# Attention part of a diffusion mixer layer in program order: a hand-written order by arrival and by k-steps in place of the scheduler's

## The chip, the cores and the metric

The kernel runs on one core of one Trainium2 chip. The metric is the device time of one execution in microseconds; the reported time is the median of 3 runs. Engines by their short names: PE (TensorE, matmuls), DVE (VectorE), ACT (ScalarE), POOL (GpSimd), SP (SyncE, which issues the DMAs).

## The reference

One layer of a hybrid backbone on 1024 sample tokens (16 rows of 64) and 128 prompt tokens, width 1024, in float32:

```python
shift, scale, gate = split(silu(cond) @ w_ada + b_ada, 3)
h = rmsnorm(x, norm_g) * (1 + scale) + shift
q, k, v, z_a, u_b, z_b, u_c, z_c, g_a, g_b, g_c = split(h @ w_in)
q, k = rmsnorm(heads(q), q_g), rmsnorm(heads(k), k_g)
y_a = attend(q, k, v)          # 8 heads of 64
y_b = fft2(u_b, positions x channels).real @ w_fnet
y_c = pooled_minus_self(u_c) @ w_pool * pool_scale
merged = (sigmoid(g_a) * ((silu(z_a) * y_a) @ p_a) + sigmoid(g_b) * ((silu(z_b) * y_b) @ p_b)
          + sigmoid(g_c) * ((silu(z_c) * y_c) @ p_c))
out = x + gate * (merged @ w_o)
```

attend is, for the sample, attention over an 8 x 16 window of the grid with a relative bias, in one softmax with 128 cached keys; for the prompt, plain softmax attention. The new k and v of the prompt are outputs too. Sample and prompt have different cond.

## The kernel before, in words

The 1152 tokens are nine tiles of 128 (tiles 0 to 7 sample, 8 prompt); names end in the tile's number. Products that need float32's precision are made of three float16 matmuls of high and low parts (hh, hl for the normalised input; wh, wl for weights): `mm3`. A "k-step" is one such triple for one of the eight 128-row slices of the input width.

1. Start. SP loads sm, then in turn pieces of w_ada (wa0 to wa15), token tiles (xt), the first weights (wr_q). For each of three groups of token tiles, ACT squares them (xsq), POOL takes the root, DVE scales, PE transposes (xt into PSUM) and ACT copies to xT. `ada_piece` runs two k-slices of w_ada's rows; `ada_end` copies a row (ar on ACT), turns it with small matmuls (pb) and DVE forms sh and gs. `h_full` applies these to xT, `scale_h` finds a power-of-two scale (ab, pbd, m1h, pbs, hm, shs), `make_h` splits to hh (ACT) and hl (DVE). `head_scales` and `v_scales` bound the cached keys and values (km and vm on DVE; pkm, pks, pvm, pvs on PE).
2. Weights come by a generator (`prep_pair`, `prep_m`): load (wr), squares for a scale (wjk on ACT), a matmul over partitions (pw), wsc on DVE and POOL, then wh on ACT and wl on DVE. Who calls the generator's next step sets when each is issued.
3. Projection of q, k, v, by pairs of heads (four pairs). Per tile a PSUM bank p collects 8 k-steps. `p1_evac` squares (sq, ACT), sums (ss, DVE), takes the root and multiplies by the gain (rs, rg on POOL) and splits v. `p1_norm` multiplies (tk, DVE) and splits into tok (high part on ACT, low part on DVE). It is called one tile later through the list `late`. Pair 0's first five tiles ("early") run k by k with h being made.
4. Attention, 72 items (pair, head, row block or prompt, column block), software-pipelined: `stage_a` scores s, then sn with the bias and mn (DVE), `stage_b` exp (ACT) and ri (DVE), `stage_c` transposes (pt), pts high part (ACT) and low part (DVE), `stage_d` product po and yt (DVE), `stage_e` transpose to yT. Between the stages `fill` takes k-steps of the next pair from the generator `p1_tiles`; after pair 3 the k-steps are those of u (`u_tiles`). `group_q` and `group_k` transpose tokens to q and keys; bias tiles are made by POOL from gt and mk; SP makes vw and kb by copies. A list `ev` of step numbers says when each helper (pair_loads, pair_cached, next_step of the weights) is called.
5. After attention: z, the Fourier and pooling branches, gates and output. It is not edited but for its PSUM banks.

Each engine's order before is set by the tile scheduler, which places the instructions that the program gives it. PSUM has eight banks: p1 2, s 2, pt 2, po 2.

Of the kernel before, what the change touches and what calls it, by code (L numbers as in the profile page):

```python
# [20 lines left out]
P = 128  # L21
# [18 lines left out]
def mixer_layer(ctx: ExitStack, tc: tile.TileContext, xs, xp, smalls, qgrow, kgrow, bgate, wss, wgate, w1, w3, pw, wo,  # L40
# [27 lines left out]
    def squares(pool, raws, name):  # L68

        ss = pool.tile([P, len(raws)], F32, tag="wss", name=f"wss_{name}", bufs=3)  # L70
        for i, r in enumerate(raws):
            n = r.shape[-1]
            jk = pool.tile([P, 1024], BF16, tag="wjk", name=f"wjk_{name}{i}", bufs=1)
            S.activation(jk[:, :n], r, AF.Square, scale=1.0 / 16384, accum_out=ss[:, i:i + 1])
        return ss

# [4 lines left out]
    def scale_of(pool, ss, pk, name):  # L81


        n = ss.shape[-1]
        T.matmul(pk, onesp, ss, start=True, stop=True)
# [3 lines left out]
        G.tensor_tensor(sc_[:, 0:1], sc_[:, 2:3], mhalf[:, 0:1], op=ALU.pow)  # L89
        pow2(sc_[:, 0:1])  # L90
# [10 lines left out]
    def prep(pieces, name):  # L101
# [73 lines left out]
    with tc.tile_pool(name="hp", bufs=1, side="right") as hp:  # L175
# [23 lines left out]
        def m_ahead(i, c):  # L199
# [18 lines left out]
        with tc.tile_pool(name="qkv", bufs=1) as qkv:  # L218
# [6 lines left out]
            def new_pair(p, wu):  # L225
# [22 lines left out]
            def p1_evac(c, t, pt):  # L248
                p = c["p"]
                sq = qkv.tile([P, 256], F32, tag="sq", name=f"sq{p}_{t}", bufs=1)  # L250
                S.activation(sq, pt[:, :256], AF.Square, scale=c["i8"])
                ss = qkv.tile([P, 4], F32, tag="ss", name=f"ss{p}_{t}", bufs=3)
                V.reduce_sum(ss, sq.rearrange("p (g d) -> p g d", d=64), axis=AX.X)
                rs = qkv.tile([P, 4], F32, tag="rs", name=f"rs{p}_{t}", bufs=3)
                G.tensor_scalar(rs, ss, EPS, None, op0=ALU.add)
                G.tensor_tensor(rs, rs, mhalf, op=ALU.pow)  # L256
                rg = qkv.tile([P, 4, 64], F32, tag="rg", name=f"rg{p}_{t}", bufs=2)
                G.tensor_tensor(rg, c["g"], rs.unsqueeze(2).to_broadcast([P, 4, 64]), op=ALU.mult)  # L258
# [7 lines left out]
                return rg  # L266

            def p1_norm(c, t, pt, rg):
                p = c["p"]
                tk = qkv.tile([P, 256], F32, tag="tk", name=f"tk{p}_{t}", bufs=2)  # L270
                tkv = tk.rearrange("p (g d) -> p g d", d=64)
                V.tensor_tensor(tk, pt[:, :256], rg.rearrange("p g d -> p (g d)"), op=ALU.mult)  # L272
# [7 lines left out]
                V.tensor_tensor(t16[:, :, 1], tkv, t16[:, :, 0], op=ALU.subtract)  # L280
                c["toks"][t] = t16

            late = []

            def p1_tiles(c, tiles, wu):

                p = c["p"]
                for t in tiles:
                    pt = bank({8: "po", 6: "s"}.get(t, "p1") if p == 0 else "p1", f"p1_{p}_{t}")
                    for k in range(KT):  # L290
                        p1_mm(pt, t, wu, k, k == 0, k == KT - 1)
                        if k == 6 and late:
                            p1_norm(*late.pop())
                        if k == KT - 1:
                            late.append((c, t, pt, p1_evac(c, t, pt)))
                        yield


            with tc.tile_pool(name="st", bufs=1) as st:
# [15 lines left out]

                pc = bank("po", "pc")
# [1286 lines left out]
```

## Time and profile before

| | us |
|---|---|
| median of 3 runs (lowest, highest) | 1007.76 (1006.62, 1008.19) |
| the profiled execution's own time | 1007.29 |
| its span in the trace | 1005.5 |
| PE busy in the span | 913.6 |
| DVE, ACT, POOL busy | 651.4, 490.6, 207.0 |
| granted clock of PE, mean | 0.971 |

A busy time is the sum of an engine's instructions in the span. The span leaves out 1.8 us of the execution. Rows of a trace give the start in us from the span's start, the duration, the engine, the line, output<-inputs, and in brackets how long the engine was idle before and what released it. A granted clock of 0.50 is half the full one.

### The profile page before, as it was taken

To read this page: it belongs to the slowest core of one execution; us is meant where nothing else is said; L and a number is where in the kernel's file an instruction comes from. 1 tells how busy PE (TensorE), PEld (TensorE's weight loads), DVE (VectorE), ACT (ScalarE), POOL (GpSimd) and SP (SyncE) were. 2 spreads that over 40 slices of the span, in tenths; PEclk is the share of its full clock that TensorE was granted. 3 is DMA by queue.
4 is the path that set the end of the run, shared out by engine and by line. 5 is a ranking of instruction groups with operands and counts; after the bars stand their busy time and mean duration, and the time that the engine had idled before them with its cause. 6 is when DMAs were issued, how large, how long until landed. Compare 5 with 4: busy or idle time off the path is not lost.

```text
span 1005.5 us, 17517 instructions
## 1 busy us (share of the span) xinstructions
PE 913.6 (91%) x6526; PEld 676.4 (67%) x6526; DVE 651.4 (65%) x1446; ACT 490.6 (49%) x1017; POOL 207.0 (21%) x354
## 2 busy tenths in 40 slices
PE   5649688888889999989989999999999999999998
PEld 1325345556556666656788669888888888877886
DVE  1246546677666665398564649888888879766322
ACT  3484546656566665446344634564545544442100
POOL 0001534544444321022200230003011030100000
PEclk9768789999999999999999999999999999999999
DMA  7733231330411321512299712363434432228321
GB/s 301 284 119 89 65 96 42 101 78 25 104 51 43 82 87 53 171 44 74 63 310 295 264 40 94 114 199 118 145 102 130 132 107 86 61 73 301 107 83 52
DMA packets 71174, 120.28 MB, mean 120 GB/s; under 512 B 11520, under 2 KB 40108, under 8 KB 71089
## 3 DMA queue, kind: packets, MB, share of 16 engines
q1 hardware_dynamic: 71089, 119.17, 37.4%
q8 instruction: 51, 0.84, 0.3%
q14 instruction: 34, 0.28, 0.1%
HBM read 85.84 MB, written 26.75 MB: 112 GB/s over the span
## 4 chain that ended last, share of the span: by engine, by line
PE 62%; DVE 13%; POOL 8%; DMA 6%; ACT 6%; issue 3%; SPq 2%; ACTq 0%; DVEq 0%; POOLq 0%
PE wo L144 3%; PE wo L146 3%; PE wo L145 3%; POOL rs L256 3%; PE xc L146 3%; PE xb L144 3%; PE xb L145 3%; PE xb L146 3%; PE xc L144 3%; PE xc L145 3%; PE xa L144 3%; PE xa L146 3%; PE xa L145 3%; POOL rg L258 2%; PE ppa L144 2%
## 5 line engine op out<-in xcount | busy, mean ns | idle before, releaser
L144 PE MATMUL p<-wh_q,hh 128*128 128x384 f16 x288 | 97.5, 339 | 4.9 <-DVE tk L272 4.9
L145 PE MATMUL p<-wl_q,hh 128*128 128x384 f16 x288 | 97.5, 338 | 0.0
L146 PE MATMUL p<-wh_q,hl 128*128 128x384 f16 x288 | 97.0, 339 | 0.0
L674 ACT ACTIVATE sn<-sn,mn 128x512 f32<-128x512 f32 x64 | 46.4, 725 | 26.7 <-DVE mn L663 26.0
L144 PE MATMUL wo<-woh,mh 128*128 128x512 f32 x144 | 56.8, 395 | 1.1 <-ACT woh L1319 1.1
L145 PE MATMUL wo<-wol,mh 128*128 128x512 f32 x144 | 56.6, 393 | 0.0
L146 PE MATMUL wo<-woh,ml 128*128 128x512 f32 x144 | 56.5, 392 | 0.0
L687 DVE TENSOR_TENSOR pts<-pt,pts 128x512 f16<-128x512 f32 (+1 forms) x72 | 46.0, 639 | 13.0 <-ACT pts L686 13.0
L272 DVE TENSOR_TENSOR tk<-p,rg 128x256 f32<-128x256 f32 x36 | 15.2, 424 | 53.6 <-POOL rg L258 53.6
L703 PE MATMUL po<-vw,pts 128*128 128x64 f16 x576 | 33.1, 193 | 17.4 <-DVE pts L687 13.3
L703 PEld LDWEIGHTS <-pts 128*128 128x128 f16 x792 | 33.7, 98 | 22.4 <-DVE pts L687 15.8
L663 DVE CUSTOM_DVE_ANT_0 sn<-s,bias 128x512 f32<-128x512 f32 x64 | 43.8, 684 | 5.6 <-PE s L659 5.5
L1485 DVE TENSOR_TENSOR yo<-wo,gb 128x512 f32<-128x512 f32 x18 | 12.4, 691 | 51.3 <-PE wo L146 51.3
L144 PEld LDWEIGHTS <-hh 128*128 128x128 f16 x288 | 29.3, 102 | 23.1 <-DVE tk L272 5.3
L88 POOL TENSOR_SCALAR wsc_g<-wsc_g 128x1 f32<-128x1 f32 x12 | 2.8, 230 | 203.8 <-DVE wsc_g L87 203.8
L279 ACT CAST tok<-tk 128x256 f16<-128x256 f32 x36 | 14.6, 405 | 60.1 <-DVE tk L272 60.0
L146 PEld LDWEIGHTS <-hl 128*128 128x128 f16 x288 | 29.1, 101 | 20.6 <-issue 3.0
L146 PEld LDWEIGHTS <-wl_m 128*128 128x128 f16 x288 | 28.2, 98 | 21.0 <-DVE wl_m L99 2.6
L684 PE MATMUL pt<-ident,sn 128*128 128x128 f32 x256 | 38.8, 274 | 3.7 <-DVE pts L687 3.2
L145 PEld LDWEIGHTS <-hh 128*128 128x128 f16 x288 | 29.1, 101 | 18.5 <-issue 3.1
L144 PEld LDWEIGHTS <-wh_m 128*128 128x128 f16 x288 | 28.7, 100 | 18.0 <-issue 1.3
L145 PEld LDWEIGHTS <-wh_m 128*128 128x128 f16 x288 | 28.2, 98 | 17.4 <-issue 0.5
(656 smaller groups left out, 3058.0 us busy)
## 6 DMA issues: line engine op xcount, KB each, us to landing
wa<-in_wss_dram SPq DMA_DIRECT2D x16, 512.0 KB, 8.4
wr_q<-in_w_dram SPq DMA_DIRECT2D x16, 384.0 KB, 3.8
wr_m<-in_w_dram SPq DMA_DIRECT2D x24, 256.0 KB, 3.0
pp_c<-pec SPq DMA_DIRECT2D x24, 192.0 KB, 4.9
pp_b<-peb SPq DMA_DIRECT2D x24, 192.0 KB, 2.9
pp_a<-pea SPq DMA_DIRECT2D x24, 192.0 KB, 1.8
ppxc<-pp_c SPq DMA_DIRECT2D x16, 288.0 KB, 3.0
ppxb<-pp_b SPq DMA_DIRECT2D x16, 288.0 KB, 3.0
```

The source lines that it names most:

```text
L144: T.matmul(out, lh, rh, start=first, stop=False)
L145: T.matmul(out, lh, rl, start=False, stop=False)
L146: T.matmul(out, ll, rh, start=False, stop=last)
L256: G.tensor_tensor(rs, rs, mhalf, op=ALU.pow)
L258: G.tensor_tensor(rg, c["g"], rs.unsqueeze(2).to_broadcast([P, 4, 64]), op=ALU.mult)
L272: V.tensor_tensor(tk, pt[:, :256], rg.rearrange("p g d -> p (g d)"), op=ALU.mult)
L279: S.copy(t16[:, :, 0], tkv)
L663: V.tensor_tensor_reduce(out=sn, in0=pS, in1=bt.rearrange("p a b -> p (a b)"), op0=ALU.add, op1=ALU.min, scale=1.0, scalar=3e38, accum_out=mn)
L674: S.activation(e[:, :n], it["sn"], AF.Exp, bias=it["mn"], scale=-1.0, accum_out=sm_)
L684: T.transpose(pt[:, j * P:(j + 1) * P], it["e"][:, j * P:(j + 1) * P], ident)
L687: V.tensor_tensor(pts[:, 1, :n], pt[:, :n], pts[:, 0, :n], op=ALU.subtract)
L703: T.matmul(po[:, :64], it["pts"][:, a, j * P:(j + 1) * P], it["vl"][j][:, c_ * 64:(c_ + 1) * 64], start=(j == 0 and i == 0), stop=(j == nk ...
```

## The change

From the start of the projection stage to the end of attention, a `manual_schedule` block makes each engine take its instructions in the order of the program, and that program is rewritten:

- The start is written out by the order in which data is to arrive. Copies of x go to DVE and ACT by turns, ar3 stands behind two casts wh_q, not four; `head_scales` and `v_scales` come in the early tiles after k = 2 and 3; the generator of weights yields after each square, matmul and root.
- `p1_evac`, `p1_norm` and `late` become `p1_done` with a clock of k-steps (`tick`, `later`): roots (ss, rs, rg) 1 step after a tile, tk `wait` steps after (8 for pair 0, 6 for the others), tok's parts 1 and 2 steps later.
- PSUM banks p1 3, s 2, pt 1, po 2 until attention ends, then 2 each; buffers sq 2, rg 3, tk 3, grow 2, kh and kl by head 2, ut 2. Late tiles of pair 0 take pt, po, p1, p1. A bias tile is made one item ahead.
- In an item, `stage_b` stands ahead of the k-steps and the low part of pts after `stage_d`. 21 steps of pair 1 (13 before) are run ahead of the first item; LEAD is 17 (16).

```diff
-    BANKS = {"p1": 2, "s": 2, "pt": 2, "po": 2}
+    banks("psa", p1=3, s=2, pt=1, po=2)
...
+            def later(d, f, *a):
+                steps["todo"].setdefault(steps["n"] + max(1, d), []).append((f, a))
+            def tick():
+                steps["n"] += 1
+                for f, a in steps["todo"].pop(steps["n"], ()):
+                    f(*a)
+            def p1_done(c, t, pt, wait):
...
+                S.activation(sq, pt[:, :256], AF.Square, scale=c["i8"])
+                S.activation(c["v"][:, t, :, 0, :], pv, AF.Copy, scale=c["sv"])
+                def roots():
+                    V.reduce_sum(ss, sq.rearrange("p (g d) -> p g d", d=64), axis=AX.X)
+                    G.tensor_scalar(rs, ss, EPS, None, op0=ALU.add)
+                    G.tensor_tensor(rs, rs, mhalf, op=ALU.pow)
+                    G.tensor_tensor(rg, c["g"], rs.unsqueeze(2).to_broadcast([P, 4, 64]), op=ALU.mult)
...
+                n = steps["n"]
+                steps["pool"] = at = max(n + wait, steps["pool"] + wait // 2 + 1)
+                later(1, roots)
+                later(at - n, normed)
+                later(at - n + 1, first_part)
+                later(at - n + 2, second_part)
...
-                        if k == 6 and late:
-                            p1_norm(*late.pop())
+                        tick()
                         if k == KT - 1:
-                            late.append((c, t, pt, p1_evac(c, t, pt)))
+                            p1_done(c, t, pt, wait)
...
+            man = ExitStack()
+            man.enter_context(tc.manual_schedule())
...
+                        pt = bank(("s", "pt", "s")[k % 3], f"xt{k}_{ts[0]}")
+                        (V.tensor_copy if k % 2 == 0 else S.copy)(xT[:, k, ts[0] * P:ts[0] * P + n], pt[:, :n])
...
-                            gen = p1_tiles(c, (8, 5, 6, 7), wu)
+                            gen = p1_tiles(c, (8, 5, 6, 7), wu, {8: "pt", 5: "po", 6: "p1", 7: "p1"}, 8)
...
-                fill(32 + 13)
-                LEAD = 16
+                fill(32 + 21)
+                LEAD = 17
...
                         stage_a(it)
+                    if 0 <= j + 1 < len(items):
+                        stage_b(items[j + 1])
                     fill(min(1, q))
                     if 0 <= j - 2 < len(items):
                         stage_e(items[j - 2])
-                    if 0 <= j + 1 < len(items):
-                        stage_b(items[j + 1])
                     if 0 <= j < len(items):
                         stage_c(items[j])
                     if 0 <= j - 1 < len(items):
                         stage_d(items[j - 1])
+                    if 0 <= j < len(items):
+                        stage_c2(items[j])
+                    if j + 3 in bias_at:
+                        p, b = bias_at[j + 3]
+                        bias_tile(pairs[p], p, *b)
                     fill(q - 1)
...
+            man.close()
+
+        banks("psb", p1=2, s=2, pt=2, po=2)
```

ACT near the end of the start, before (wh_q0 are the first weights' high parts, ar3 the last row of w_ada's product, wjk_q1 the squares of the next weights):

```order
L74 ACTIVATE wjk_q03_413,wss_q0_406<-wr_q03_299 128x768
L98 ACTIVATE wh_q00_422<-wr_q00_293,wsc_q0_417 128x768
L98 ACTIVATE wh_q01_426<-wr_q01_295,wsc_q0_417 128x768
L98 ACTIVATE wh_q02_430<-wr_q02_297,wsc_q0_417 128x768
L98 ACTIVATE wh_q03_434<-wr_q03_299,wsc_q0_417 128x768
L370 COPY ar3_447<-pa3_438 128x512
L74 ACTIVATE wjk_q10_841,wss_q1_840<-wr_q10_764 128x768
```

Here ar3 stands behind all four casts.

ACT at the same place now:

```order
L87 ACTIVATE wjk_q03_415,wss_q0_408<-wr_q03_170 128x768
L113 ACTIVATE wh_q00_435<-wr_q00_164,wsc_q0_428 128x768
L113 ACTIVATE wh_q01_439<-wr_q01_166,wsc_q0_428 128x768
L415 COPY ar3_445<-pa3_421 128x512
L113 ACTIVATE wh_q02_473<-wr_q02_168,wsc_q0_428 128x768
L113 ACTIVATE wh_q03_477<-wr_q03_170,wsc_q0_428 128x768
L468 ACTIVATE hh0_95<-xT_121,shs_77 128x1152 x3
```

The row ar3 has gone from behind four casts to behind two, and the casts wh_q02 and wh_q03 stand where the next weights' squares stood.

DVE at the same place, before (sh and gs are the shift and scale from pb3; km and vm the maxima of the cached keys and values):

```order
L99 SCALAR_TENSOR_TENSOR wl_q02_431<-wr_q02_297,wsc_q0_417,wh_q02_430 128x768
L99 SCALAR_TENSOR_TENSOR wl_q03_435<-wr_q03_299,wsc_q0_417,wh_q03_434 128x768
L379 TENSOR_TENSOR sh_86<-pb3_449,col_82 128x4
L380 TENSOR_TENSOR gs_85<-pb3_449,col_82 128x4
L388 TENSOR_REDUCE ab_462<-sh_86 128x1
L442 TENSOR_REDUCE km_560<-kall_458 64x8
L381 TENSOR_SCALAR gs_85<-gs_85 128x4
L426 TENSOR_REDUCE vm_577<-vall_460 128x4
L382 TENSOR_TENSOR gs_85<-gs_85,col_82 128x4
L387 TENSOR_REDUCE ab_462<-gs_85 128x1
```

All four wl_q0 stand ahead of sh, and km and vm between the steps from sh and gs to ab.

DVE at the same place now:

```order
L114 SCALAR_TENSOR_TENSOR wl_q00_436<-wr_q00_164,wsc_q0_428,wh_q00_435 128x768
L114 SCALAR_TENSOR_TENSOR wl_q01_440<-wr_q01_166,wsc_q0_428,wh_q01_439 128x768
L427 TENSOR_TENSOR sh_86<-pb3_447,col_82 128x4
L428 TENSOR_TENSOR gs_85<-pb3_447,col_82 128x4
L429 TENSOR_SCALAR gs_85<-gs_85 128x4
L430 TENSOR_TENSOR gs_85<-gs_85,col_82 128x4
L435 TENSOR_REDUCE ab_456<-gs_85 128x1
L436 TENSOR_REDUCE ab_456<-sh_86 128x1
L437 SCALAR_TENSOR_TENSOR ab_456<-ab_456 128x1
L438 SCALAR_TENSOR_TENSOR ab_456<-ab_456 128x1
L442 TENSOR_REDUCE m1h_463<-pbd_461 2x1
L444 TENSOR_SCALAR mdh_465<-ident_66,m1h_463 2x2
```

km and vm have left the chain from sh to ab, and two of the low parts wl_q0 stand behind it (rows further on).

DVE at the first items of attention, before (tk1_1 is tile 1 of pair 1; sn, ri, yt and pts belong to items):

```order
L253 TENSOR_REDUCE ss1_1_1269<-sq1_1_1267 128x4
L261 SCALAR_TENSOR_TENSOR v161_1042<-p1_1_1_1195,vf1_1034,v161_1042 128x2x64
L663 ISA sn0_0_0_0_1228,mn0_0_0_0_1222<-s0_0_0_0_1221,bias0_0_0_0_1223 128x512
L663 ISA mn0_0_0_0_1222 128x1
L676 RECIPROCAL ri0_1_2_0_1246<-sm0_1_2_0_1244 128x1
L705 TENSOR_SCALAR yt0_2_0_1318<-po0_0_2_0_1319,ri0_0_2_0_1202,vf0_596 128x64
L272 TENSOR_TENSOR tk1_1_1368<-p1_1_1_1195,rg1_1_1274 128x256
L663 ISA sn0_0_1_0_1286,mn0_0_1_0_1279<-s0_0_1_0_1278,bias0_0_1_0_1280 128x512
L663 ISA mn0_0_1_0_1279 128x1
L676 RECIPROCAL ri0_0_0_0_1311<-sm0_0_0_0_1309 128x1
L687 TENSOR_TENSOR pts0_1_2_0_1315<-pt0_1_2_0_1313,pts0_1_2_0_1315 128x128
```

Here four rows of items lie between the split of v and tk1_1, and the next sn and the low part of pts are queued behind tk1_1.

DVE at the same place now, from the split of v of tile 2 (which follows its sum ss1_2) to its tk:

```order
L303 SCALAR_TENSOR_TENSOR v161_1040<-p1_1_2_1260,vf1_1032,v161_1040 128x2x64
L743 ISA sn0_1_0_0_1383,mn0_1_0_0_1380<-s0_1_0_0_1379,bias0_1_0_0_1352 128x512
L743 ISA mn0_1_0_0_1380 128x1
L756 RECIPROCAL ri0_0_1_0_1387<-sm0_0_1_0_1385 128x1
L787 TENSOR_SCALAR yt0_2_0_1345<-po0_1_2_0_1399,ri0_1_2_0_1295,vf0_636 128x64
L770 TENSOR_TENSOR pts0_0_0_0_1397<-pt0_0_0_0_1392,pts0_0_0_0_1397 128x512
L743 ISA sn0_1_1_0_1421,mn0_1_1_0_1418<-s0_1_1_0_1417,bias0_1_1_0_1405 128x512
L743 ISA mn0_1_1_0_1418 128x1
L756 RECIPROCAL ri0_1_0_0_1425<-sm0_1_0_0_1423 128x1
L787 TENSOR_SCALAR yt0_0_0_1442<-po0_0_0_0_1443,ri0_0_0_0_1334,vf0_636 128x64
L770 TENSOR_TENSOR pts0_0_1_0_1440<-pt0_0_1_0_1435,pts0_0_1_0_1440 128x512
L306 TENSOR_TENSOR tk1_2_1363<-p1_1_2_1260,rg1_2_1362 128x256
```

Ten rows, the DVE part of two whole items, now lie between the split of v and tk1_2, and the low part of each item's pts stands right behind yt, with no tk between them.

More of the change, by code (lines that the diff above doesn't have):

```diff
@@ L89, in scale_of @@
         G.tensor_tensor(sc_[:, 0:1], sc_[:, 2:3], mhalf[:, 0:1], op=ALU.pow)
+        return sc_
+    def scale_of(pool, ss, pk, name):
+        T.matmul(pk, onesp, ss, start=True, stop=True)
+        sc_ = scale_root(pool, pk, name)
         pow2(sc_[:, 0:1])
@@ L110, in prep @@
         yield unit
-        ss = squares(wp, raws, name)
+        ss = wp.tile([P, len(raws)], F32, tag="wss", name=f"wss_{name}", bufs=3)
+        for i, r in enumerate(raws):
+            square(wp, ss, r, i, name)
+            yield unit
+        pk = bank("po", f"pw_{name}")[:, :len(raws)]
+        T.matmul(pk, onesp, ss, start=True, stop=True)
         yield unit
-        pk = bank("po", f"pw_{name}")
-        sc_ = unit["sc"] = scale_of(wp, ss, pk[:, :len(raws)], name)
+        sc_ = unit["sc"] = scale_root(wp, pk, name)
         unit["inv"] = sc_[:, 1:2]
+        yield unit
+        pow2(sc_[:, 0:1])
         if "ready" in h_scale:
@@ L494, in mixer_layer @@
                 pts = [bank(ebank[t], f"p1_0_{t}") for t in range(early)]
-                for k in range(KT):
+                for k in range(6):
+                    for t in range(early):
+                        p1_mm(pts[t], t, wu, k, k == 0, False)
+                    if k == 0:
+                        make_h(1)
+                        h_full(6, V)
                     if k == 1:
-                        h_full(6, V)
+                        make_h(2)
+                        h_full(7, S)
+                    if k + 2 < KT and k > 1:
+                        make_h(k + 1)
                     if k == 2:
-                        h_full(7, S)
-                    make_h(k)
-                    if k < 6:
-                        for t in range(early):
-                            p1_mm(pts[t], t, wu, k, k == 0, False)
-                    if k == 3:
                         v_bound(hm)
                         head_scales(kall)
+                    if k == 3:
                         v_scales(vall)
+                    if k == 5:
+                        make_h(7)
                         c0 = new_pair(0, wu)
@@ L745, in mixer_layer @@
                 pairs = [c0, None, None, None]
+                BIASES = []
+                for hd, rb, cb in ORDER:
+                    if rb < 2 and (hd, rb, CTYPE[cb]) not in BIASES:
+                        BIASES.append((hd, rb, CTYPE[cb]))
+                first_use = [min(i for i, (hd, rb, cb) in enumerate(ORDER) if rb < 2 and (hd, rb, CTYPE[cb]) == b) for b in BIASES]
+                bias_at = {p * NI + f: (p, b) for p in range(4) for f, b in zip(first_use, BIASES)}
                 nextw = {}
```

283 lines of the change are left out of this document (158 added, 125 removed).

## The prediction

> **What bounds the kernel now.** I read the page's busy shares and slices first, then the chain, then the span cut into its stages, and the waits inside two stages.
>
> ```profile
> PE 913.6 (91%) x6526; PEld 676.4 (67%) x6526; DVE 651.4 (65%) x1446; ACT 490.6 (49%) x1017; POOL 207.0 (21%) x354
> PE   5649688888889999989989999999999999999998
> PEclk9768789999999999999999999999999999999999
> PE 62%; DVE 13%; POOL 8%; DMA 6%; ACT 6%; issue 3%; SPq 2%; ACTq 0%; DVEq 0%; POOLq 0%
> ```
>
> TensorE is busy 913.6 of 1005.5 us, so at most 92 us of idle time, and what is run at a low clock, can be won by moving instructions. The slices put most of it in the first 16 (25 us each): the change's region. The chain still gives 38% to other engines, 8% to POOL, which is busy for 21% only: the kernel waits there on latency, not on work. The stages (times from the span's start; then busy time with count of PE, PEld, DVE, ACT, POOL; granted clock; DMA share; GB/s):
>
> ```profile
> 0.00:76.30 76.30, 40.41 (x178) 19.12 (x178) 21.85 (x69) 42.24 (x80) 5.86 (x21) 0.80 0.63 232
> 76.30:98.30 22.00, 22.00 (x123) 12.68 (x123) 16.60 (x39) 11.57 (x16) 1.50 (x3) 0.90 0.30 86
> 98.30:104.40 6.10, 6.09 (x39) 3.52 (x36) 2.54 (x6) 2.17 (x6) 5.35 (x9) 1.00 0.53 148
> 104.40:142.10 37.70, 24.56 (x128) 13.87 (x129) 20.55 (x65) 17.89 (x40) 16.82 (x27) 0.77 0.28 78
> 142.10:413.80 271.70, 246.87 (x2267) 167.84 (x2265) 176.95 (x544) 169.00 (x420) 107.73 (x211) 0.99 0.24 67
> 413.80:700.00 286.20, 273.76 (x1730) 218.75 (x1729) 205.56 (x401) 139.70 (x287) 43.66 (x54) 0.99 0.46 151
> 700.00:1005.50 305.50, 299.89 (x2072) 240.57 (x2069) 207.30 (x326) 108.04 (x169) 26.06 (x30) 1.00 0.37 115
> ```
>
> 76.3 is the first matmul of the projection (p), 98.3 to 104.4 the end of the five early tiles, 104.4 where PE next stands, 142.1 the first score matmul (s), 413.8 the end of attention. PE's idle time by stage is span less busy: 35.9 at the start, 0 in the early tiles, 13.1 in the rest of pair 0 (104.4 to 142.1), 24.8 in attention, 18.1 after it. Only the first four are ordered anew; the last, in two rows, keeps its scheduler and its work.
>
> **Part 1, the start.** The change gives half of the transposes' copies to DVE, puts ar3 behind two wh_q casts instead of four, and km and vm (the bounds for the caches) behind the sh-to-shs chain. Rows on the path to 76.3:
>
> ```profile
> L353 ACT COPY xT<-xt 128x384 f32<-128x384 f32 x24 | 9.7, 507 | 15.3 <-PE xt L352 15.3
> 61.20 0.59 PE L85 MATMUL pw_q<-wss_q,onesp 128*128 128x4 f32 x2 [4.33 <-ACT wjk_q L74]
> 63.19 3.41 ACT L98 ACTIVATE wh_q<-wr_q,wsc_q 128x768 f16<-128x768 f32 x4 [2.04 <-DVE wsc_q L79]
> 67.12 1.87 PE L373 MATMUL pb<-pick,ar 128*128 128x2 f32 x8 [3.47 <-ACT ar L370]
> 69.31 1.20 DVE L442 TENSOR_REDUCE km<-kall 64x8 f32<-64x1024 f32 x1
> 70.50 0.67 DVE L426 TENSOR_REDUCE vm<-vall 128x4 f32<-128x512 f32 x1
> 76.30 0.50 PE L144 MATMUL p<-wh_q,hh 128*128 128x384 f16 x1
> ```
>
> The chain is squares (wjk), pw_q, wh, ar, pb, sh and gs, shs, first p. ACT loses 12 of 24 copies: 12 x 0.41 (9.7/24) = 4.9, which I take in full, since ACT is what pw_q waited for (4.33). Two casts out of the way of ar3: 3.41/2 = 1.7. km and vm out of the chain: 1.20 + 0.67 = 1.9. Sum 8.5, first p at about 68.
>
> Part is given back at once. DVE, in order, now writes two wl_q halves before the first low part of h, and head and value scales stand inside the early tiles, where PE, in order, meets their small matmuls:
>
> ```profile
> L421 DVE SCALAR_TENSOR_TENSOR hl<-xT,shs,hh 128x1152 f16<-128x1152 f32 x8 | 10.8, 1401 | 0.0
> L99 DVE SCALAR_TENSOR_TENSOR wl_q<-wr_q,wsc_q,wh_q 128x768 f16<-128x768 f32 x4 | 3.8, 1013 | 1.0 <-ACT wh_q L98 1.0
> 30.00 1.97 PE L352 MATMUL xt<-ident,xt 128*128 128x128 f32 x8 [5.45 <-DVE xt L336]
> ```
>
> Two wl_q are 3.8/2 = 1.9 of PE waiting; pks and pvs cost PE the reductions ahead of them, 1.2 and, with the chain behind vm, about 1.5: 4.6 together, and 0.9 more of low clock, since waits now stand inside these tiles (0.90 over 22 us lost 2.2 before). Net gain 3. Ends: +8.5 if nothing is given back; -2.5 if an x group or a piece of w_ada that comes late makes PE, which now can't take the other first, stand once more as long as the x transposes did at 30.00 (5.45). SP's loads up to vall keep their order. Behind them the weights of pair 2 move from ahead of the masks to step 18 of pair 1, behind a store and two copies that wait for their data; they are wanted some 40 steps (19 us) later, so I cost it 0, and at worst one such wait of 5.45, which is inside the ends of parts 2 and 3.
>
> **Part 2, the rest of pair 0.** Here PE stands still while one tile's chain runs (squares on ACT, ss on DVE, rs and rg on POOL, tk on DVE, tok on ACT and DVE), since the next transposes need its tokens. Waits of PE, then three slices of 5 us with their clock:
>
> ```profile
> PE pq L573 <- DVE tok L280: 6.1, 3, 3.0
> PE p L144 <- DVE tk L272: 4.9, 1, 4.9
> PE pk L588 <- DVE tk L272: 2.1, 1, 2.1
> 110.00:115.00 5.00, 3.84 (x16) 2.14 (x16) 3.34 (x12) 1.81 (x5) 2.48 (x5) 0.53 0.07 23
> 125.00:130.00 5.00, 5.00 (x32) 3.00 (x31) 4.37 (x8) 3.19 (x7) 1.25 (x2) 1.00 0.64 211
> 135.00:140.00 5.00, 3.46 (x11) 1.64 (x12) 1.97 (x7) 1.40 (x4) 2.49 (x4) 0.52 0.45 105
> ```
>
> The five waits are the whole 13.1. At full clock a matmul takes 5.00/32 = 0.156 us, a k-step (three) 0.47. The four late tiles get a bank each (pt, po, p1, p1), tk comes 8 steps after its tile (3.8 us of matmuls between), q and k transposes follow at fixed steps, and 21 instead of 13 steps of pair 1 are run before the first score. So the 13.1 idle has matmuls to fill it: 8 more steps are 24 matmuls, 3.8 us, taken out of attention (so no gain by themselves), and the other steps stand where the chains run. The low clock lost (1 - 0.77) x 24.56 = 5.6 more. Of 13.1 + 5.6 = 18.7 I keep 4.3 as lost: pw_q of pair 1 stands in PE's order close behind its squares (2.2, half of the 4.33 that the first one stood for four squares), and the last tile's tok before its transposes (2.1, the mean wait above, 2.6, less one step). Gain 14.4. Ends: 6, if waits of 7 remain and the clock stays low; 18.7.
>
> By the Trainium skill, "TensorE: Matmul & The Clock Gate", Part 1, the clock falls to half after an idle window of about 3.4 us and comes back after as long a busy one. The trace agrees as far as it goes: 0.53 and 0.52 stand beside waits of 3.0 and 4.9. By that rule the 5.6 comes back only if no wait of over some 3 us is left; with one left, the part is 14.4 - 2.8 = 11.6.
>
> **Part 3, attention.** The waits from 142.1 to 413.8, with the two POOL rows of one tile ahead of them (a wait: engine, line, releaser: us, times, longest):
>
> ```profile
> 104.43 1.04 POOL L256 TENSOR_TENSOR rs<-rs,mhalf 128x4 f32<-128x4 f32 x1
> 105.55 0.61 POOL L258 TENSOR_TENSOR rg<-grow,rs 128x256 f32<-128x256 f32 x1
> ...
> DVE tk L272 <- POOL rg L258: 37.8, 24, 2.5
> PE po L703 <- DVE pts L687: 13.7, 15, 3.0
> PE pt L684 <- DVE pts L687: 3.2, 4, 1.1
> PE po L703 <- DVE wsc_q L87: 2.6, 2, 1.5
> ```
>
> The tk row is the cause of the next two: DVE stands in front of tk until POOL has rg, and the low part of pts (which po needs) is queued behind tk. On POOL rs and rg are 1.04 + 0.61, to which a short add comes: under 2 us from ss to rg. tk now stands at least 5 steps (2.35) behind ss, and where a score, its transposes or its product fall between, more. The wait at tk goes (37.8 to near 0), and with it most of 13.7 + 3.2 = 16.9 of PE's. The new waits, worked out: at the three changes of pair the first weights and bias rows are a DMA and a chain away, 3 x 1.5 (longest of the wsc_q row) = 4.5; bias tiles, now made one item ahead instead of when a buffer comes free, hold POOL, which is busy 107.7 of 271.7, but not PE. Of the 24.8 idle, 7.9 never was of this kind (24.8 - 16.9): it stays, and with the 4.5 some 12 remain. Gain 12.8. Ends: 0 and 20. What stalls next if tk doesn't is pts again, by the transposes' single bank. One item without a stall:
>
> ```profile
> 396.93 0.38 PE L659 MATMUL s<-ka,q 128*128 128x512 f16 x1
> 397.67 0.69 DVE L663 CUSTOM_DVE_ANT_0 sn<-s,bias 128x512 f32<-128x512 f32 x1 [0.37 <-PE s L659]
> 397.96 0.60 PE L684 MATMUL pt<-ident,sn 128*128 128x128 f32 x4
> 398.66 0.25 PE L703 MATMUL po<-vw,pts 128*128 128x64 f16 x3
> 398.95 0.34 DVE L705 TENSOR_SCALAR yt<-po,ri,vf 128x64 f32<-128x64 f32 x1 [0.58 <-PE po L703]
> 399.73 0.69 DVE L687 TENSOR_TENSOR pts<-pt,pts 128x512 f16<-128x512 f32 x1 [0.31 <-ACT pts L686]
> 400.21 0.38 PE L659 MATMUL s<-ka,q 128*128 128x512 f16 x1
> ```
>
> The item takes 400.21 - 396.93 = 3.28 us. pts is done at 400.42 and the next pt would start at 400.21 + 1.03 = 401.24: a slack of 0.82 us. Items with more steps in them have more. I cost the single bank at 0 on average; its cover is this 0.82.
>
> **Part 4, after attention.** New banks as before, the same code: a shift. 0, between -3 and 3 (PE is 96% and 98% busy there; a transfer that isn't earlier can take some back, and DVE is no less loaded).
>
> **Sum.** 3 + 14.4 + 12.8 + 0 = 30.2. The profiled execution took 1007.29 us (its span 1005.5 and 1.8 around it), 0.5 below the median of 1007.76. 1007.3 - 30.2 = 977.1 by the profiled one; against the median 977.6.
>
> **Rivals.**
> A, nearly all idle time goes: +8.5, +18.7, +20 give 47: 961. For it: PE had work ready in all these places. Against: an order written by hand leaves a wait wherever an arrival is late, and no engine can step round it.
> B, in-order waits eat half: start -2.5, pair 0 +6, attention +8.5 (half of 16.9): 12, so 996. For it: DVE is busy 177 of 272 us in attention, so that any of its waits holds s, yt and pts; the tk row shows what one misplaced wait costs.
> C, slower, by the single bank of pt: pt of the next item waits for pts of this one, which now stands behind yt (which waits for po) and behind anything the steps put on DVE. If pts is late by d against the row above, each of 72 items costs d - 0.82. With two writes of wl_q (2 x 1.01) in front of it in 48 items it is 1.2 x 48 = 58, less 30: 1035. It decides from a mean lateness of 0.82 + 30.2/72 = 1.24 us. For it: DVE has at least 0.69 + 0.34 + 0.69 = 1.7 us of work for each item (sn, yt, pts) and the weights on top. Against: the weights' writes stand singly between the items' steps.
> D, the order doesn't matter because the time saved is waited for after attention (weights by DMA): that needs transfers that were just in time at 413.8, while DMA's share in attention is 0.24. About 1007.
>
> **Numbers.** Forecast (966 to 988) 0.56; A 0.12; B (988 to 1003) 0.18; D 0.03; C and other losses 0.11. What a measurement can tell from no change is about 0.2%, 2 us. Faster 0.56 + 0.12 + 0.18 = 0.86, same 0.03, slower 0.11. The range 963 to 1002 leaves out some 0.07 below and 0.13 above; the likeliest case alone is 966 to 988.
>
> **What would show it.** First p at 66 to 70, and PE waits of 4 to 5 inside the early tiles. The first s at 126 to 132 with 24 more p matmuls ahead of it, and the clock near 1.00 from 100 on. In attention the row of tk waiting for rg gone, PE idle near 12 of some 255 us, its end near 383. After it 592 us as before. I am wrong if pt waits for pts in most items (C), if waits of over 3 us with a clock near 0.5 remain before the first s (B), or if the time from the end of attention to the end grows.

## The result: 1020.4 us, slower by 1.3%, and the profile after

The changed kernel takes 1020.38 us (median of 4 runs, 1017.86 to 1024.52) against 1007.98 for the kernel before: the ratio is 1.0126, with a 95% interval of 1.0089 to 1.0163. 977.6 was forecast. The page of the profiled execution (1020.7 us, its span 1018.8):

```profile
PE 913.4 (90%) x6526; PEld 677.1 (66%) x6526; DVE 661.2 (65%) x1461; ACT 483.4 (47%) x1003; POOL 206.5 (20%) x353
PE   4678858868869989988989999999999999999998
PEclk9759979979989999999999999999999999999999
PE 65%; DVE 11%; ACT 7%; DMA 7%; issue 5%; POOL 4%; SPq 1%; ACTq 0%; DVEq 0%; POOLq 0%
```

The work is the same (PE 913.4 us against 913.6), and POOL's share of the chain fell from 8% to 4%, as the removed wait at tk would have it. But the dips in PE's slices have moved: they now stand in the slices at 127 to 153, 204 to 229 and 280 to 306 us, and the clock dips with them. The stages, cut at the first p (65.8), at 104 (104.4 in the prediction's table), the first score (128.3) and the first matmul after attention (425.3):

```profile
0.00:65.80 65.80, 36.86 (x174) 20.56 (x174) 25.70 (x67) 31.03 (x54) 5.29 (x17) 0.77 0.68 257
65.80:104.00 38.20, 34.37 (x191) 19.34 (x191) 28.29 (x73) 19.86 (x37) 11.58 (x19) 0.90 0.19 53
104.00:128.30 24.30, 20.36 (x140) 12.26 (x138) 14.45 (x42) 12.96 (x27) 12.63 (x19) 0.93 0.24 56
128.30:425.30 297.00, 248.31 (x2231) 165.77 (x2229) 180.26 (x555) 170.73 (x428) 107.86 (x218) 0.94 0.26 72
425.30:1018.80 593.50, 573.52 (x3799) 459.13 (x3797) 412.52 (x726) 248.80 (x460) 69.09 (x81) 1.00 0.41 133
```

The first score comes at 128.3 instead of 142.1: 13.8 us won. Attention takes 297.0 instead of 271.7: 25.3 lost. What follows takes 593.5 instead of 591.7. -13.8 + 25.3 + 1.8 = +13.3, which is the difference of the spans (1018.8 - 1005.5). In attention PE stands for 297.0 - 248.3 = 48.7 us, where 24.8 were before and 12 were forecast. The waits in it (the last row is DVE's at tk, 37.8 us before):

```profile
PE s L739 <- DMA kb<-ka: 27.2, 4, 11.4
PE pt L764 <- DVE pts L770: 13.9, 19, 1.5
PE py L796 <- DVE yt L787: 3.6, 3, 1.8
PE s L739 <- ACT ka L675: 2.4, 3, 0.9
...
DVE tk L306 <- POOL rg L302: 2.3, 2, 1.6
```

The first row is the new one: 27.2 us in four waits, one at the start of each pair's attention (11.43, 7.25, 6.11 and 2.43), where it was 0.9 in three. The second row holds most of what stood at po and pt before: 13.7 + 3.2 = 16.9 us then, 13.9 now.

A score is two matmuls into one bank, one that reads the keys ka and one that reads kb, which holds the same keys with their high and low halves swapped. kb is made from ka by SP's copies, the last four of a pair in one go: the first two of them fill key columns 512 to 767, the other two 1024 to 1279. The first score of a pair reads columns 0 to 1023 (r0 = 0 and 16 rows of 64 in the kernel), so the second of the four copies is the last that it needs. At the start of pair 1 before (the start, the duration, the engine):

```profile
212.09 0.61 PE L588 MATMUL pk<-id,tok 128*128 128x128 f16 x8
214.14 1.02 ACT L595 COPY ka<-pk 128x1024 f16<-128x1024 f16 x1
215.19 0.66 SPq L579 DMA_DIRECT2D kb<-ka  x1
215.61 0.38 PE L659 MATMUL s<-ka,q 128*128 128x512 f16 x1
215.90 0.63 SPq L580 DMA_DIRECT2D kb<-ka  x1
217.22 0.61 SPq L580 DMA_DIRECT2D kb<-ka  x1
218.25 0.38 PE L659 MATMUL s<-kb,q 128*128 128x512 f16 x1
```

and the same place after:

```profile
205.83 0.61 PE L668 MATMUL pk<-id,tok 128*128 128x128 f16 x8
206.74 1.01 ACT L675 COPY ka<-pk 128x1024 f16<-128x1024 f16 x1
206.83 0.68 SPq L600 DMA_DIRECT2D gt<-in_rpbp_dram  x1
207.80 0.38 PE L739 MATMUL s<-ka,q 128*128 128x512 f16 x1 [0.87 <-ACT ka L675]
208.10 0.67 SPq L659 DMA_DIRECT2D kb<-ka  x1
208.82 0.61 SPq L660 DMA_DIRECT2D kb<-ka  x1
210.12 0.60 SPq L660 DMA_DIRECT2D kb<-ka  x1
215.43 0.61 PE L739 MATMUL s<-kb,q 128*128 128x512 f16 x1 [7.25 <-DMA kb<-ka]
```

Before, 2.6 us with other work lie between the two halves of the score, and 6.2 between pk and the half that reads kb; no wait for kb is shown there. The second copy was issued at 215.90 and read 2.35 us later. After, the two halves follow each other, nothing but a step lies between pk and them, and PE stands for 7.25 us until the second copy, issued at 208.82, has landed: 6.61 us from issue to score. PE's order says so: the k-steps between pk and the first half that reads kb are, for pairs 0 to 3, 9.3, 4.0, 5.3 and 5.7 before, and 6, 1, 1 and 1 after.

### The profile page after: what moved, and what is told of

Its sections match the earlier page's. It is cut to its first block, busy times and chain, and to the rows that moved or that the text cites. A ratio compares the mean times of both kernels' runs of the same rounds, so it can differ in the third digit from the quotient of the medians.

```text
span 1018.8 us, 17538 instructions
## 1 busy us (share of the span) xinstructions
PE 913.4 (90%) x6526; PEld 677.1 (66%) x6526; DVE 661.2 (65%) x1461; ACT 483.4 (47%) x1003; POOL 206.5 (20%) x353
## 4 chain that ended last, share of the span: by engine, by line
PE 65%; DVE 11%; ACT 7%; DMA 7%; issue 5%; POOL 4%; SPq 1%; ACTq 0%; DVEq 0%; POOLq 0%
PE wo L165 3%; PE wo L167 3%; PE wo L166 3%; PE xc L167 3%; PE xb L165 3%; PE xb L166 3%; PE xb L167 3%; PE xc L165 3%; PE xc L166 3%; PE xa L165 3%; PE xa L167 3%; PE xa L166 3%; PE p L167 2%; PE p L165 2%; PE p L166 2%
## 5 line engine op out<-in xcount | busy, mean ns | idle before, releaser
L766 ACT CAST pts<-pt 128x512 f16<-128x512 f32 (+1 forms) x72 | 39.7, 552 | 30.1 <-PE pt L764 28.5
L764 PE MATMUL pt<-ident,sn 128*128 128x128 f32 x256 | 39.1, 275 | 14.0 <-DVE pts L770 13.9
L739 PE MATMUL s<-kb,q 128*128 128x512 f16 x64 | 25.2, 394 | 27.2 <-DMA kb<-ka 27.2
L167 PEld LDWEIGHTS <-hl 128*128 128x128 f16 x288 | 29.2, 101 | 22.5 <-issue 3.2
L764 PEld LDWEIGHTS pt<-ident,sn 128*128 128x128 f32 x256 | 29.1, 141 | 21.7 <-issue 17.4
L165 PEld LDWEIGHTS <-hh 128*128 128x128 f16 x288 | 29.4, 102 | 19.9 <-issue 2.5
L300 POOL TENSOR_SCALAR rs<-ss 128x4 f32<-128x4 f32 x36 | 8.4, 233 | 167.0 <-DVE ss L299 166.4
L165 PEld LDWEIGHTS <-wh_m 128*128 128x128 f16 x288 | 28.8, 100 | 18.2 <-issue 1.8
L166 PEld LDWEIGHTS <-wh_m 128*128 128x128 f16 x288 | 28.3, 98 | 17.6 <-issue 0.8
```

What stands on the lines that cost most here:

```text
L165: T.matmul(out, lh, rh, start=first, stop=False)
L166: T.matmul(out, lh, rl, start=False, stop=False)
L167: T.matmul(out, ll, rh, start=False, stop=last)
L739: T.matmul(pS, c["q"][rb][:, hd, bs], kx[:, hd].rearrange("p (r c) -> p r c", c=64)[:, r0:r0 + 16, KC0[cb]:KC0[cb] + 32], start=(i == 0), ...
L764: T.transpose(pt[:, j * P:(j + 1) * P], it["e"][:, j * P:(j + 1) * P], ident)
L766: S.copy(pts[:, 0, :n], pt[:, :n])
```

## The experiments

All times are medians; the ratio is to the kernel before on the same chip. "Score" is the first score, "end" the first matmul after attention, kb and pt the waits of PE for the copies kb and of pt for pts, in us from each run's profile.

| kernel | us | ratio (95%) | score | end | kb | pt |
|---|---|---|---|---|---|---|
| before | 1007.98 | 1 | 142.1 | 413.8 | 0.9 | 3.2 |
| after | 1020.38 | 1.0126 (1.0089 to 1.0163) | 128.3 | 425.3 | 27.2 | 13.9 |
| no_manual | 1016.23 | 1.0076 (1.0047 to 1.0104) | 138.3 | 421.2 | 2.8 | 29.4 |
| start_only | 1005.74 | 0.9987 (0.9971 to 1.0003) | 127.8 | 411.9 | 1.8 | 30.4 |
| kb_first | 1022.83 | 1.0155 (1.0114 to 1.0196) | 128.6 | 426.0 | 7.7 | 15.0 |
| two_pt | 1022.10 | 1.0134 (1.0092 to 1.0177) | 131.9 | 423.5 | 19.3 | 0 |
| kb_loads | 1012.70 | 1.0060 (1.0038 to 1.0082) | 129.4 | 414.9 | 7.6 | 13.5 |
| two_pt_w4 | 1010.46 | 1.0033 (1.0009 to 1.0057) | 131.4 | 412.3 | 27.0 | 0 |
| kb_two_pt | 1002.45 | 0.9936 (0.9913 to 0.9959) | 132.2 | 408.2 | 8.1 | 0 |
| start_two_pt | 1004.57 | 0.9975 (0.9955 to 0.9995) | 129.9 | 407.7 | 2.0 | 0 |
| kb_act | 1024.40 | 1.0158 (1.0128 to 1.0189) | 131.7 | 427.7 | 20.3 | 16.5 |
| kb_early | 990.13 | 0.9825 (0.9783 to 0.9866) | 132.8 | 393.9 | 8.2 | 0 |
| kb_early_act | 992.55 | 0.9836 (0.9803 to 0.9868) | 135.3 | 397.1 | 0 | 0 |
| early_one_pt | 993.96 | 0.9854 (0.9826 to 0.9882) | 127.5 | 396.7 | 4.5 | 17.1 |
| vw_last | 1000.48 | 0.9935 (0.9916 to 0.9954) | 128.4 | 401.5 | 0 | 0 |
| pk_early | 997.93 | 0.9916 (0.9896 to 0.9937) | 128.1 | 400.2 | 9.1 | 14.3 |
| lead16 | 1015.16 | 1.0083 (1.0056 to 1.0111) | 128.2 | 421.1 | 36.6 | 4.7 |

A 0 means that the profile has no such wait.

**Whose order.** Two kernels take the written order away, in all of the region or from the end of the early tiles on:

```diff
-            man.enter_context(tc.manual_schedule())
```
(no_manual; in start_only `man.close()` stands ahead of the attention part instead.)

> The changed program without manual_schedule, so that the scheduler orders it as before. Theory K (PE, in program order, stands at a score s until the swapped keys kb have come by SP's copies, 27.2 us in the changed kernel; a scheduler would put other matmuls there): the row of s waiting for kb falls from 27.2 to under 5 us and the time to 985 to 1000 us. Theory P (the rewritten steps and the single bank pt cost it, whoever orders them): the time stays at 1012 to 1025 us and pt still waits for pts some 14 us.

> manual_schedule ends after the early tiles, so pair 0's rest and attention are ordered by the scheduler, with the changed program. Start's term as measured (first p at 65.8 instead of 76.3) kept: like no_manual or better, 985 to 998 us by theory K. If the start's gain is taken back later or the attention part's steps are at fault: 1008 or more.

The kb row falls as theory K has it, to 2.8 and 1.8. The scheduler puts 5.7 to 6.0 k-steps between pk and kb's half in pairs 1 to 3 of the same program. But the time doesn't follow: pt now waits for pts. The row of PE's waits in no_manual (sum, count, longest):

```profile
PE pt L763 <- DVE pts L769: 29.4, 26, 2.8
```

and in start_only:

```profile
PE pt L765 <- DVE pts L771: 30.4, 25, 2.8
```

Rival C's place, the single bank, is real: some 30 us here, half of the 58 that I gave it at most. The wait that the change was to remove is back in both: in attention DVE stands at tk for rg for 43.1 us in no_manual and 41.9 in start_only (37.8 before, 2.3 in the changed kernel). start_only keeps the start's gain (score at 127.8) and loses it in attention (284.1 us, 271.7 before): it ends level with the kernel before.

**The copies' place on SP.** kb_first moves the next pair's loads, and in pair 1 the 16 copies vw, behind the copies kb, and the steps that use those loads with them; kb_loads puts vw behind the weights as well. The edit of kb_first (d is 6 for p == 1):

```diff
-                            at_(10, pair_loads, c)
-                            at_(18, next_load)
...
+                            at_(21 if p == 1 else 15, pair_loads, c)
+                            at_(22 if p == 1 else 18, next_load)
...
-                            at_(4, windows, b)
...
+                            at_(15 + d if p == 1 else 4, windows, b)
```

> The changed kernel with the loads of the next pair (kr, vr, gt, wr_q), and in pair 1 the 16 copies vw, moved behind the copies kb on SP. Theory K: the first wait of s for kb falls from 11.4 to about 2 us, the later ones from 7.3 and 6.1 to about 5, 27.2 in all to 12 to 15, and with the half clock behind the first wait the time falls by 13 to 20 us, to 1000 to 1007. Theory P: kb's wait is only the place where the lateness shows; its time turns up as waits of pt, po or DVE, and the total stays within 5 us of 1020.

> As kb_first, but on SP behind the copies kb of pair 0 come first the next pair's loads (kr, vr, gt), then the weights wr_q, and only then the 16 copies vw, since in kb_first ACT stood 11.6 us for wr_q behind them and PE 12.5 us at py. Theory S (SP, which takes 0.6 to 0.8 us for each issue and goes in program order, is what PE ends up waiting for at the start of each pair): kb waits near 8 us as in kb_first, no wait of PE over 3 us between 128 and 160 us, the last po at 400 to 406 and the time 1000 to 1006. Theory P (lateness only moves from one wait to another): 1015 or more.

In both the kb row falls to under 8. So some 19.5 of the 27.2 us came from what stood ahead of kb on SP; the 7.7 that are left in kb_first (0.3 in pair 0, with six steps behind pk, and 2.4 to 2.5 in the others, with one) are the bare chain of issue and landing. kb_first gains no time by it, for one wait took another's place:

```profile
147.07 2.03 SPq L123 DMA_DIRECT2D wr_q<-in_w_dram  x4
150.56 0.84 ACT L87 ACTIVATE wjk_q<-wr_q 128x768 bf16<-128x768 f32 x1 [11.64 <-DMA wr_q<-in_w_dram]
153.91 0.48 PE L796 MATMUL py<-ident,yt 128*128 128x128 f32 x1 [12.46 <-DVE yt L787]
```

The 16 copies vw hold SP for 12 us, the weights behind them come late, and ACT, which in program order stands at their square, holds exponents and pts behind it, then DVE, then PE. With the weights ahead of vw (kb_loads) the same place costs 4.4 us at py, and the time falls by 7.7 us: less than the 14 to 20 expected.

**The banks.** two_pt takes two banks pt and two p1; two_pt_w4 also calls tk 4 steps behind its tile instead of 6; kb_two_pt is this with kb_loads.

```diff
-    banks("psa", p1=3, s=2, pt=1, po=2)
+    banks("psa", p1=2, s=2, pt=2, po=2)
-                ebank = ["p1", "p1", "p1", "s", "s"]
+                ebank = ["p1", "p1", "pt", "s", "s"]
-                            gen = p1_tiles(c, (8, 0, 1, 2, 3, 4, 5, 6, 7), wu, {}, 6)
+                            gen = p1_tiles(c, (8, 0, 1, 2, 3, 4, 5, 6, 7), wu, {}, 4)
```

> The changed kernel with two banks pt and two p1 (the third early tile takes pt). Theory P: pt no longer waits for pts (13.9 us to under 2) and the time falls by 12 us or more, to below 1009. Theory K: the pt row goes too, but part of it is taken up by the waits for kb; 3 to 10 us, 1010 to 1017.

> As two_pt (two banks pt, two p1), with tk 4 steps behind its tile instead of 6 in pairs 1 to 3, since in two_pt the 13.9 us of pt came back as 13.7 us of the projection p waiting for tk to free one of its two banks. Theory B (a bank is short wherever it is taken from, and 2 steps earlier free it in time): the row of p waiting for tk falls to under 4 us, DVE waits for rg again for some 5 us in all, the time 1008 to 1015. If tk then stands in front of rg as before the change (37.8 us): 1020 or more.

> kb_loads and two_pt_w4 together. If theories S and B both hold the two gains add: PE's waits in attention under 20 us, the last po at 390 to 396, the time 988 to 998. If either only moves the lateness on: over 1005.

In two_pt the pt row goes and the projection waits for its own banks instead, as long as before (the row below); the time stays at 1022.1 though the kb row is 7.9 us shorter. With 4 steps 1.9 us of this row are left in two_pt_w4, a gain of 9.9 us. In attention DVE then waits for rg for 18.2 us again, and PE 4.8 at po for pts. The row of two_pt:

```profile
PE p L165 <- DVE tk L306: 13.7, 10, 2.1
```

kb_loads (-7.7) and two_pt_w4 (-9.9) add up to kb_two_pt (-17.9) within the intervals: no interaction of the two shows here. Its ratio is 0.6% below 1 and clear of noise, though the time is not in the 988 to 998 expected.

**The scheduler with two banks.**

> As start_only (the scheduler orders everything behind the early tiles), with two banks pt and two p1 instead of one and three. In start_only pt waited 30.4 us for pts. Theory B: that row falls to 3 to 5 us as in the kernel before, the time to 980 to 992. If the 30.4 stands beside other waits, or p's banks take its place: 998 or more.

A miss: 1004.6. The lateness of pts stays and shows at po:

```profile
PE po L786 <- DVE pts L771: 24.6, 26, 2.6
```

What the trace shows on DVE is the old wait: in attention it stands at tk for rg for 43.4 us, more than the 37.8 before. So the scheduler seems not to keep tk as far behind its tile as the program writes it, and pts is late as before the change; no run tried to hold tk there.

**Who issues the copies.** In kb_act only the issuer of kb is another: ACT, right behind its copy to ka.

```diff
-                        swapped(c["kb"][:, :, b], c["ka"][:, :, b])
+                        swapped(c["kb"][:, :, b], c["ka"][:, :, b], nc.scalar)
```

> The changed kernel with one edit: the swapping copies kb are issued by ACT, right behind its own copy to ka, instead of by SP; no other order is touched. Theory S (SP's order holds kb): the row of s waiting for kb falls from 27.2 to 8 to 12 us (four copies issued and landing, at each pair), the time by 10 to 20 us, to 1000 to 1010. Theory L (SP isn't late: the copies land late because the DMA queues carry gt and wr_q): the row stays above 20 and the time above 1014.

The first wait falls from 11.4 to 3.1. In the changed kernel ACT had written ka by 129.55 and SP issued the first copy at 137.55, 8.0 us later; ACT issues it at once. So most of that wait was SP's queue, though the copy then takes longer to be read (7.21 us from issue, 5.02 in the changed kernel). In pairs 1 and 2 SP was late by 0.4 us or less, and the waits stay:

```profile
204.47 0.67 SPq L600 DMA_DIRECT2D gt<-in_rpbp_dram  x1
205.97 0.62 ACTq L660 DMA_DIRECT2D kb<-ka  x1
213.63 0.58 PE L739 MATMUL s<-kb,q 128*128 128x512 f16 x1 [7.93 <-DMA kb<-ka]
```

From the second copy's issue to the score it is 7.66 us here and 6.61 in the changed kernel (215.43 - 208.82), with the 496.5 KB of gt issued ahead. In kb_first, with gt behind, it is 2.21:

```profile
210.75 0.64 SPq L660 DMA_DIRECT2D kb<-ka  x1
212.96 0.38 PE L739 MATMUL s<-kb,q 128*128 128x512 f16 x1 [2.53 <-DMA kb<-ka]
```

So theory L holds for pairs 1 and 2 and theory S for most of pair 0's wait. The time doesn't follow the row: the first score comes 3.4 us later and pt's row grows by 2.6.

**The distance on PE.** pk_early is one edit: the last keys' transposes stand ahead of the queries', 8 (pair 0) or 5 steps earlier; in pair 0 the queries' come 3 steps earlier too.

```diff
-                            d = 6 if p == 1 else 0
-                            at_(11 + d, group_q, b, 1)
-                            at_(14 + d, group_k, b, 1)
+                            d = 3 if p == 1 else 0
+                            at_(9 + d, group_k, b, 1)
+                            at_(11 + d, group_q, b, 1)
```

> The changed kernel with one edit: the transposes of a pair's last keys (pk) stand ahead of those of the queries and 8 (pair 0) or 5 steps earlier, so that 14 and 6 k-steps of the projection lie between pk and the score that reads kb, where 6 and 1 lay. Loads, vw and banks are untouched. Theory D (the distance on PE is too short for the copy to ka, four copies on SP and their landing): waits for kb fall from 27.2 to 6 to 12 us and the time to 1000 to 1010. Theory S (the queue on SP ahead of kb decides): the row stays above 18 and the time above 1012.

> The changed kernel with LEAD 16 instead of 17, as before the change: items come one later against the k-steps, so 4, 3 and 2 k-steps lie between pk and the score that reads kb in pairs 1 to 3 (1 each in the changed kernel), 6 in pair 0 as now. Theory D: the waits of pairs 1 to 3 fall from 7.3, 6.1, 2.4 to about 5, 4 and 1, the first one stays near 11; the time falls by 5 to 9 us, to 1011 to 1015. Theory S: within 3 us of 1020.

pk_early gives 22.5 us, the most of any single edit; the kb row falls to 9.1, and the clock in attention is 0.99 again (0.94 in the changed kernel). What is left is mostly pair 0's wait of 4.99, where gt still stands ahead of kb and 0.57 follows at 136.6 to 142.0. The edit holds both causes: in pairs 1 and 2 it also puts kb ahead of gt on SP, so it doesn't say how much is distance alone. lead16 shows that distance alone isn't enough. There 4, 3 and 2 steps lie between, and the row rose to 36.6, against theory D, because two loads gt now stood ahead of kb in pairs 1 and 2:

```profile
199.54 0.67 SPq L600 DMA_DIRECT2D gt<-in_rpbp_dram  x1
201.87 0.67 SPq L600 DMA_DIRECT2D gt<-in_rpbp_dram  x1
...
214.33 0.61 PE L739 MATMUL s<-kb,q 128*128 128x512 f16 x1 [8.78 <-DMA kb<-ka]
```

It still is 5 us faster: pt's row fell by 9.2 (4.7 instead of 13.9), about as much as kb's rose, and the small rows of py, ka, pqz and pw_q from 7.5 to 2.0.

**Together.** early_one_pt loads pair 2's weights and pair 1's keys at steps 0 and 1 of pair 1, puts vw behind kb there, and has pk_early's edit. kb_early has two_pt_w4's banks besides, kb_early_act issues kb from ACT, vw_last puts vw behind kb in all pairs and pair 0's tile 6 in a bank s.

> kb_two_pt with the order on SP set otherwise: pair 2's weights and pair 1's kr, vr, gt are loaded at steps 0 and 1 of pair 1, keys are transposed before the queries and 3 to 8 steps earlier, vw goes behind kb in pair 1. Theory S: the rest of kb's wait (8.1) and the wait of 5.8 us behind ACT's square of late weights go, PE idles 12 to 16 us in attention and the time is 984 to 994. If these waits come back at vw, pt or tk: 1000 or more.

> kb_early with kb issued by ACT. If SP still holds kb in kb_early: faster than it by 2 to 6 us. If ACT, which feeds pts and the exponents, loses more by four issues at each pair than PE gains: within 2 us or slower.

> kb_early with the banks and the 6 steps of the changed kernel (one bank pt, three p1): the order on SP and of the keys alone. If SP's order and the banks are independent shares of the lost time, and the banks are worth 10 us as in two_pt_w4: 998 to 1002 us, pt waiting some 14 us for pts. If the banks matter less once the keys are in time: 990 to 995. If the early keys need the second bank: over 1006.

> kb_early with the 16 copies vw behind kb and the loads in all pairs, and pair 0's tile 6 in a bank s, so that pair 1's first tile needn't wait for tile 6 to be normalised. Theory S: the three waits of s for kb that are left (2.5 to 3.0 us) fall to under 1 each and the 1.9 us of p waiting for tk goes; 982 to 988 us. If vw or wr_q then comes late, po or ACT waits for them and the time is 990 or more.

kb_early takes 990.13 us, 30 less than the changed kernel and 1.75% less than the one before. early_one_pt comes to 993.96 without the banks: with the keys in time the banks are worth about 4 us, not 10, and the two intervals overlap. Taking kb's last waits away didn't pay: from ACT (kb_early_act) it costs as much as it gains, and in vw_last the lateness moves on to the next transfer behind vw. yT has one buffer, its store is issued behind vw, and ACT's next write to it stands in front of pts:

```profile
209.25 0.53 SPq L803 DMA_DIRECT2D yT_d<-yT  x1
214.71 0.27 ACT L798 COPY yT<-py 128x128 f32<-128x128 f32 x1 [10.48 <-DMA yT_d<-yT]
215.52 0.29 PE L785 MATMUL po<-vw,pts 128*128 128x64 f16 x2 [9.70 <-ACT pts L766]
```

kb_early's attention for comparison (idle 23.3 of 261.1, clock 1.00):

```profile
132.80:393.90 261.10, 237.78 (x2231) 163.77 (x2229) 180.65 (x555) 168.00 (x428) 110.22 (x221) 1.00 0.27 75
```

Its idle time is still 23.3 us, against 24.8 before the change: po waits 7.9 us for pts, s 8.2 for kb. The lowest of any run is kb_early_act's 20.0, so the 12 us of the forecast were not reached by any order tried. kb_early's gain is the earlier first score (9.3 us) and an attention 10.6 us shorter, of which 1.5 are idle time; the rest is busy time (2231 matmuls instead of 2267, and clock 1.00 instead of 0.99). 3.7 us are lost again after attention.

## Why the prediction was wrong, step by step

- **Parts 1 and 2 (the start and pair 0): right, in part by luck.** First p at 65.8 (66 to 70 forecast), waits of 3.1 in the early tiles (4.6 counted), the first score at 128.3 (126 to 132). 13.8 us and the 24 matmuls moved ahead (3.8) make 17.6; 3 + 14.4 = 17.4 was the sum. The split was off both ways: the projection's 120th matmul, which ends five tiles of 24, starts at 92.62 instead of 98.16 (where my table had the tiles end at 104.4), a gain of 5.5 and not 3, which leaves 12.1 and not 14.4 for the rest of pair 0. There the clock was 0.93 from 104 to 128.3, not near 1.00, and one wait of 2.80 stood before pair 0's transposes of the prompt.
- **Part 3, the wait at tk: right, but not what it frees.** 37.8 became 2.3, and po's wait for pts went (13.7 before, no row after). Most of 16.9 at po and pt was to go with it; 13.9 of it came back at pt.
- **Part 3, the gain of 12.8: wrong, and this is the step that failed.** Forecast were 271.7 - 12.8 - 3.8 = 255.1 us for attention; it took 297.0. Of these 41.9, 36.7 are idle time (48.7, not 12). The largest term, 27.2 at kb, had no place in the sum: its 4.5 for the changes of pair stood for weights and bias rows, and of SP's order only the move of pair 2's weights was costed, "0, and at worst one such wait of 5.45". The copies kb, and the loads gt that now stood just ahead of them, are not in the prediction, and they made four waits of up to 11.4. The rows that would have told are in the trace of the kernel before. The score's two halves stood apart on PE, by one to five k-steps, and even so the second copy at pair 1 was issued at 215.90, landed after 2.0 us and was read at 218.25: 0.35 us to spare. And one copy of pair 2, issued right behind gt and four loads of weights, took 6.5 us to land, with no one waiting for it then (two rows, and the landing times of kb's copies):

```profile
253.96 0.68 SPq L528 DMA_DIRECT2D gt<-in_rpbp_dram  x1
255.44 0.60 SPq L580 DMA_DIRECT2D kb<-ka  x1
DMA to landing us min/median/max: 2.0/2.4/6.5
```

I compared DVE's order with care and took PE's as unchanged, where a move by a few rows was the largest part of the loss. The wait for rg that I looked at lay on an engine with slack; kb lay on the engine without.
- **The single bank of pt: mis-sized.** Costed at 0 with a slack of 0.82 us for each item; it measured 13.9 us, at 19 of 72 items, 0.7 each. That is rival C's mechanism below its price: it made part of the loss and didn't decide, since early_one_pt is faster than the kernel before with 17.1 us of it. "Slower" had a chance of 0.11, given for this mechanism and others not named; kb was one of the latter.
- **The clock: not in the sum at all for attention.** It stood at 0.99 before and at 0.94 after. Around the waits (the stretch; its length, the busy time of PE, PEld, DVE, ACT and POOL, the granted clock, the DMA share and GB/s):

```profile
143.20:146.00 2.80, 2.75 (x9) 1.42 (x10) 1.35 (x6) 0.87 (x3) 0.00 (x0) 0.50 0.00 0
146.00:150.00 4.00, 4.00 (x20) 2.04 (x19) 3.24 (x13) 1.90 (x7) 0.00 (x0) 0.71 0.00 0
160.00:200.00 40.00, 33.99 (x331) 23.05 (x331) 29.62 (x92) 24.20 (x55) 18.33 (x34) 1.00 0.14 33
215.40:218.00 2.60, 2.57 (x19) 1.81 (x20) 1.35 (x5) 0.75 (x3) 0.56 (x2) 0.50 0.95 356
218.00:220.00 2.00, 2.00 (x9) 0.91 (x7) 0.54 (x2) 0.49 (x2) 1.92 (x4) 0.51 0.15 60
359.00:362.60 3.60, 0.62 (x3) 0.01 (x1) 0.81 (x2) 2.24 (x5) 1.22 (x3) 1.00 0.32 97
364.40:366.60 2.20, 2.20 (x13) 1.11 (x11) 1.20 (x3) 1.33 (x4) 0.75 (x2) 0.50 0.00 0
```

Behind the waits of 11.43 (ends at 143.25) and 7.25 (215.43) PE works at half clock for some 5 us; between them, where no wait is over 1.5, it has 1.00. So such a wait costs more than itself, by an estimate from these rows 2.75 x 0.50 + 4.00 x 0.29 = 2.5 us for the first and 2.57 x 0.50 + 2.00 x 0.49 = 2.3 for the second. The Trainium skill, "TensorE: Matmul & The Clock Gate", Part 1, puts the fall behind an idle window of about 3.4 us; the trace agrees for these two. Behind the fourth wait, of 2.43 us (ends at 362.66), the clock fell too; there PE had been busy for 0.62 of the 3.60 us from 359.0 on, so a stretch of low work was enough, without 3.4 us of full idleness.
- **Part 4: right in size.** 593.5 against 591.7 (within 3).
- **The rivals.** B (in-order waits eat the gain) named the kind of loss, but at DVE, where kb's is at PE, and was priced at 996. The range's upper end of 1002 held one wait of 5.45 and not 27.2 us in four.

## What to carry to other kernels

When an order is written by hand, list for each reader on the busiest engine what produces its operand, and count the work between them on that engine against the whole chain, each copy's issue and its landing behind the loads ahead of it included. What landed just in time before is the next wait once the engine runs denser. Of a queue that serves everything in turn (SP here), order small urgent copies ahead of large loads, and re-read who stands next in it after every move.

## What the runs showed of the hardware that I had not expected

- A small copy issued right behind one 496.5 KB load is read late. From its issue to the score that waits for it: 6.61 and 5.78 us in the changed kernel (pairs 1 and 2), 6.55 to 7.66 in kb_act, 4.84 in lead16's pair 3, where gt stands between vw and kb, against 2.13 in the changed kernel's, where it stands ahead of vw; 9.83 and 9.39 in lead16's pairs 1 and 2 behind two such loads; and 2.10 to 2.21 in all pairs of kb_first, where none is issued within 10 us ahead of it. Issued by another engine (kb_act) it is no faster.
- The 16 copies vw of one pair hold SP for 12.48 us, 0.78 each, and everything else that SP issues stands behind them:

```profile
115.83 12.48 SPq L697 DMA_DIRECT2D vw<-v  x16
```
